# Two layout edits, five more side-by-side products per MLP, a split bias table and a final layer norm that works in PSUM

## The chip, the cores and the metric

The kernel runs on one NeuronCore of one Trainium2 chip. The time is device microseconds of that core, from launch to end; lower is better. Runs are shown as medians, and the profile is of one execution with its own time.

## The reference

A two-layer decoder trunk over 512 tokens of width 1024, all in float32. Layer 0 mixes with multi-head latent attention (8 heads, compressed keys and values, rotary part). Layer 1 mixes with grouped-query attention in a sliding window of 128 with a sink per head and a relative-position bias that is looked up in a 32x16 table. After each mixer and after each MLP comes a residual and a layer norm:

```python
def _mlp(x, w_up, w_down):
    h = jax.nn.relu(x @ w_up)          # 1024 -> 4096
    return (h * h) @ w_down            # 4096 -> 1024
...
for l in range(DEPTH):                 # DEPTH = 2
    y = _mla(x, ...) if l < 1 else _swa(x, ..., k_band, v_band, rel_bias)
    x = _layernorm(alpha * x + y, ln_mix_g[l], ln_mix_b[l])
    x = _layernorm(alpha * x + _mlp(x, mlp_w_up[l], mlp_w_down[l]), ln_mlp_g[l], ln_mlp_b[l])
```

The two MLPs hold most of the arithmetic.

## The kernel before, in words

**Precision.** Float32 operands are split into two parts of a reduced matmul type (fp32r): a high part `h` (ACT copies and rounds) and a low part `l` (DVE or POOL subtracts the high part from the value). A product is three passes of matmuls: high by high, high by low, low by high. `split` (lines 79 to 92) makes the parts, `three` lists the passes of one 128-row chunk, `by_pass` sorts a list of chunks by pass, and `group` (line 113) issues the matmuls and fixes their order in TensorE's program.

**The MLP.** The 4096 hidden features are worked in four blocks `q` of 1024. The up product (weights by tokens) of a block, and the down product of the first three, are done by a scheme for 2x2 block matrices that needs seven smaller products in place of eight. The products have the numbers 1, 2, 5, 3, 6, 7, 4; in the step strings `U'5` is the fifth up product of the next block and `D5` the fifth down product of this one. The order of the steps is written out in `FIRST_STEPS`, `SECOND_STEPS`, `STEPS` and `LAST_STEPS`. Blocks 2 and 3 run `U'1 D5 U'2 D3 U'5 ...`, block 0 runs `U'1 U'2 U'5 U'3 U'6 ...`. There are two MLPs, so each block occurs twice in a run. The last block's down product is done in the ordinary way (class `TokMajor`, method `finish`).

**An up product** has 128x128 weights as the stationary operand and 256 tokens of a factor of x as the moving one. Its two weights are `i`, the two halves of the output of each `j`, the chunks of the contraction `k` (4). There are two ways to issue it:

- plain (`up`): for each `(i, j, k)` three matmuls of 256 columns, 48 in all, into half a PSUM bank; `up_out` evacuates once per `i`, 512 columns at a time;
- side by side (`up_side`, lines 749 and 753): one matmul of 512 columns, the high weight by the high and the low part of x next to each other, and one of 256 columns, the low weight by the high part of x into the first half: 32 matmuls in all, one whole bank for each `(i, j)`; `side_out` (lines 786 and 787) evacuates each bank with an ACT copy of one half and a DVE add of the other.

`SIDE_BY_SIDE` says which products of which block go the second way: before, products 5 and 3 of blocks 1, 2 and 3. Products 1 and 2 share their banks (product 2 adds to what product 1 left).

**The factors of x** lie in tiles `xtb` of shape `[128, 2, 4, 256]`: part (high, low), chunk k, token. The 512-column moving operand of `up_side` is `src.both(n)[:, :, k, :]`: two runs of 256 elements, 1024 elements apart.

**Scratch.** Tag `uv` has three buffers: in block 0 two hold the sums `a` and `b` of the factors of x until the factors 6 and 7 are split, and one holds `u`. PSUM has six banks of tag `mm` and two of tag `tr`.

**The order of the work.** TensorE's matmuls and the weight loads by DMA keep program order (`keep_in_program_order`). ACT, DVE and POOL are ordered by a planner that takes ready instructions by priority from its own model of time. Each of these engines then runs its list in order.

**The bias table** (`bias_bands`, line 1032) is one plain float32 matmul of the 33x16 table by a 33x384 one-hot matrix; the result goes through DRAM and back as bands, which layer 1 reads much later.

**Values** (`values` of the first layer) are six matmuls of 512 columns for each token tile: for each of two chunks the passes high-high, high-low (low weights `wl`), low-high.

**The end.** `finish` of the last MLP evacuates the last token tile (t = 3) in chunks of 512, 256 and 256 columns: `add_last` adds the bank to x in SBUF and counts the statistics. `layer_norm` then aggregates, has POOL raise the variance to -1/2 (line 419), meanwhile subtracts the mean and multiplies by g over 1024 columns (line 442), and last multiplies by that and adds b in two halves (line 446), each followed by its DMA to the output.

Of the kernel before, what the change touches and what calls it, by code (L numbers as in the profile page):

```python
# [10 lines left out]
F32R = mybir.dt.float32r  # L11
AF = mybir.ActivationFunctionType
ALU = mybir.AluOpType
# [3 lines left out]
P = 128  # L17
D = 1024
S = 512
NT = S // P  # L20
# [6 lines left out]
SQH, SKVH, SHD = 16, 4, 64  # L27
# [6 lines left out]
BANDW = 384  # L34
POOL_O, POOL_SO = (0, 2), (0, 1, 2, 3)
WARM = 18

SIDE_BY_SIDE = {0: (), 1: (5, 3), 2: (5, 3), 3: (5, 3)}
PAIRED = (1, 2, 3, 4, 5, 6, 7)

ON_POOL = ("w_h", "w_o", "w_sq", "w_so")
# [12 lines left out]
def build(tc, nc, io, out):  # L54
    with ExitStack() as top:
        cp = top.enter_context(tc.tile_pool(name="cp", bufs=1))
        wp = top.enter_context(tc.tile_pool(name="wp", bufs=1))
        xp = top.enter_context(tc.tile_pool(name="xp", bufs=1))
# [7 lines left out]
        def nm(s):  # L66
            n_names[0] += 1
            return f"{s}_{n_names[0]}"

        def bank(cols=512, tag="mm", bufs=6):  # L70
            return ps.tile([P, cols], F32, tag=tag, bufs=bufs, name=nm(tag), padded_shape=[P, 512])
# [4 lines left out]
        def f32(ap):  # L76
            return ap.bitcast(F32)
# [23 lines left out]
        def pe(ins):  # L101
            tc.keep_in_program_order(ins)
# [3 lines left out]
        def pin(ins):  # L106

            if pinned[0]:
                pe(ins)

        def group(dst, pairs, first=True, last=True, **kw):
            for i, (st, mv) in enumerate(pairs):
                pe(nc.tensor.matmul(  # L113
                    dst, st, mv, start=first and i == 0, stop=last and i == len(pairs) - 1, **kw
                ))

        def three(sh, sl, mh, ml):
            return [(sh, mh), (sh, ml), (sl, mh)]

        def by_pass(chunks):  # L120

            return [chunk[n] for n in range(3) for chunk in chunks]
# [6 lines left out]
        def tiles_of_weights(aside=None):  # L129

            if aside:
                return aside()
            wh = wp.tile([P, 1024], F32R, tag="wh", bufs=4, name=nm("wh"))
            wl = wp.tile([P, 1024], F32R, tag="wl", bufs=4, name=nm("wl"))
            return wh, wl
# [222 lines left out]
        b = bank()  # L358
# [6 lines left out]
        def pieces(kp):  # L365
            return both[kp][:, 0:1024].rearrange("p (j c) -> p j c", j=2), both[kp][:, 1024:1664].rearrange("p (j c) -> p j c", j=2)
# [13 lines left out]
        for kp in range(4):  # L380
            x, weight = pieces(kp)
            wh, wl = tiles_of_weights()
            for j in (slice(0, 1), slice(1, 2)) if kp == 0 else (slice(0, 2),):
                w = lambda tile: tile[:, 0:640].rearrange("p (j c) -> p j c", j=2)[:, j]
                k = slice(2 * (kp % 2) + j.start, 2 * (kp % 2) + j.stop)
# [22 lines left out]
        relb = cp.tile([33, SQH], F32, name="relb")  # L408
# [14 lines left out]
        xs = [None] * NT  # L423
# [7 lines left out]
        def layer_norm(t, gb, dst, within=None):  # L431

            x = xs[t]
            mv = sp.tile([P, 2], F32, tag="mv", bufs=4, name=nm("mv"))
            pin(nc.vector.bn_aggr(mv, stats[t]))
            stats[t] = None
            v = sp.tile([P, 1], F32, tag="v", bufs=8, name=nm("v"))
            pin(nc.vector.tensor_scalar(v, mv[:, 1:2], LN_EPS, None, ALU.add))  # L438
            r = rsqrt_of(v)
            if within:  # L440
                within()
            pin(nc.vector.scalar_tensor_tensor(x, x, mv[:, 0:1], gb[:, 0, :], ALU.subtract, ALU.mult))
            n = 2 if dst is None and t == NT - 1 else 1
            for i in range(n):
                c = slice(i * D // n, (i + 1) * D // n)
                pin(nc.vector.scalar_tensor_tensor(x[:, c], x[:, c], r, gb[:, 1, c], ALU.mult, ALU.add))
                if dst is None:
                    nc.sync.dma_start(out[t * P : (t + 1) * P, c], x[:, c])
# [116 lines left out]
        stats = [None] * NT  # L565

        def count(t, c):

            n = 256 if t == NT - 1 else 512
            if stats[t] is None:  # L570
                stats[t] = sp.tile([P, D // n, 6], F32, tag="bn", bufs=4, name=nm("bn"), padded_shape=[P, 4, 6])
            for i in range(c.start // n, c.stop // n):
                pin(nc.vector.bn_stats(stats[t][:, i, :], xs[t][:, i * n : (i + 1) * n]))
# [4 lines left out]
        def add_plain(t, c, b):  # L578
            nc.vector.tensor_add(xs[t][:, c], b, xs[t][:, c])  # L579

        def add_scaled_last(t, c, b):
            add_scaled(t, c, b)
            count(t, c)

        def add_last(t, c, b):
            add_plain(t, c, b)
            count(t, c)

        def feat_major(src, w, dst, cols=slice(0, S), ks=range(KD), order=lambda chunks: sum(chunks, [])):
            wh, wl = w  # L590
# [55 lines left out]
        class XFactors(Factors):  # L646
# [6 lines left out]

            def both(self, n):
                if n not in self.tiles:
                    self.tiles[n] = xp.tile([P, 2, 4, 256], F32R, tag="xt", bufs=8, name=nm("xtb"))
                return self.tiles[n]

            def part(self, n, p):
                if n in PAIRED:  # L660
                    return self.both(n)[:, p]
                at = {1: (0, 0), 2: (0, 1), 5: (1, 0), 3: (1, 1), 6: (2, 0), 7: (2, 1), 4: (3, p)}[n]
                tile = (at[0], p if n != 4 else 0, "")
                if tile not in self.tiles:
                    self.tiles[tile] = xp.tile([P, 2, 4, 256], F32R, tag="xt", bufs=8, name=nm(("xth", "xtl")[p]))
                return self.tiles[tile][:, at[1]]
# [34 lines left out]
        def mlp(src, gb, dst, mp):  # L701
# [17 lines left out]
            class Block:  # L719
# [18 lines left out]
                def side(self, n):  # L738
                    return n in SIDE_BY_SIDE[self.q]

                def up_side(self, n, w):

                    key = own_bank.get(n, n)
                    for i, (wh, wl) in enumerate(w):
                        for j in range(2):
                            b = self.bank(("U", key), (i, j))
                            for k in range(4):
                                c = slice(j * 512 + k * P, j * 512 + (k + 1) * P)
                                pe(nc.tensor.matmul(  # L749
                                    b.rearrange("p (a b) -> p a b", a=2), wh[:, c], src.both(n)[:, :, k, :],  # L750
                                    start=n not in (2, 4) and k == 0, stop=False, skip_group_check=True,
                                ))
                                pe(nc.tensor.matmul(  # L753
                                    b[:, 0:256], wl[:, c], src.part(n, 0)[:, k, :],
                                    start=False, stop=k == 3, skip_group_check=True,
                                ))
                            self.side_out(n, i, j, b)
                        if n in (2, 6, 7, 4):
                            self.up_out(n, i)
                        if (self.q, i) == (0, 0) and n in (1, 2):  # L760
                            with tc.high_priority():
                                src.turn(n + 1)
# [155 lines left out]
            b = blocks[NFF - 1]  # L918
# [27 lines left out]
        with tc.tile_pool(name="mla", bufs=1) as mp:  # L946
# [3 lines left out]
            ckv_h = mp.tile([P, 2, S], F32R, name="ckv_h")  # L950
            ckv_l = mp.tile([P, 2, S], F32R, name="ckv_l")
# [57 lines left out]
            for kp in range(4):  # L1009
                wh, wl = weights("w_kv")  # L1010
# [16 lines left out]
            def bias_bands():  # L1027
                ohot, es = qrot[:, 0, :], qrot[:, 1, :]
                with tc.issue_after(small.ins):
                    nc.sync.dma_start(ohot[:33, :BANDW], io["oh"])  # L1030
                eb = bank()
                nc.tensor.matmul(eb[:SQH, :BANDW], relb, ohot[:33, :BANDW], start=True, stop=True)
                nc.scalar.activation(es[:SQH, :BANDW], eb[:SQH, :BANDW], AF.Copy)
                nc.sync.dma_start(ed, es[:SQH, :BANDW])
                e = ed[:, :]
                skew = bass.AP(tensor=e.tensor, offset=e.offset + 127, ap=[[BANDW, SQH], [-1, P], [1, 256]])
                nc.sync.dma_start(band, skew)
# [51 lines left out]
            def values(w, t):  # L1089
                wh, wl = w  # L1090
                tk = slice(t * P, (t + 1) * P)
                b = bank()
                for c in range(2):
                    cc = slice(c * 512, (c + 1) * 512)
                    group(b, three(ckv_h[:, c, tk], ckv_l[:, c, tk], wh[:, cc], wl[:, cc]), c == 0, c == 1)
                split(v_h[-1][:, t, :], v_l[-1][:, t, :], b)

            heads = [{} for _ in range(H)]
# [45 lines left out]
            for t in range(NT):  # L1144
                tk = slice(t * P, (t + 1) * P)
                b = bank()
                for r in range(3):
                    wh, wl = ws[r // 2]
                    c = slice((r % 2) * 512, (r % 2 + 1) * 512)
# [107 lines left out]
        gb = lambda: load_gb(io["ln_mix_g"][0], io["ln_mix_b"][0])  # L1257
# [188 lines left out]
        gb = lambda: load_gb(io["ln_mix_g"][1], io["ln_mix_b"][1])  # L1446
# [115 lines left out]
```

## Time and profile before

| what | value |
|---|---|
| median of 3 runs | 995.35 us (994.9 to 995.58) |
| profiled execution, its own time | 995.34 us |
| its span, first to last instruction | 993.1 us |
| mean granted TensorE clock | 0.998 |
| busy: PE, DVE, ACT, POOL | 983.4, 783.4, 569.7, 247.1 us |

The span is from the first to the last instruction; the 2.24 us between it and the profiled execution's time lie around it. Busy times are unions of an engine's instructions. A matmul's start is measured and its end is modelled, so what a matmul costs in a full stream is read from the distance between starts, or from the length of a piece of the chain divided by its count.

### The profile page before, as it was taken

What the parts mean: (1) busy time and instruction counts of PE and PEld (TensorE: products, weight loads), DVE (VectorE), ACT (ScalarE), POOL (GpSimd) and SP (SyncE); (2) the same over time, 40 slices, a digit from 0 to 9 for tenths busy, and PEclk for the clock granted to TensorE, in tenths of its full rate; (3) what the DMA queues carried; (4) which work ended last, traced back from release to release, by engine and by line L of the source; (5) the groups of instructions that cost most, each with busy time, mean ns of one, the idle gap of its engine ahead of it and who ended that gap; (6) DMA issues with size and microseconds to landing.
All of it is one profiled execution on the core that took longest, in us unless ns stands there. A gap on an engine that the chain in (4) does not pass through costs nothing.

```text
span 993.1 us, 15619 instructions
## 1 busy us (share of the span) xinstructions
PE 983.4 (99%) x5944; PEld 880.0 (89%) x5944; DVE 783.4 (79%) x1288; ACT 569.7 (57%) x895; POOL 247.1 (25%) x267
## 2 busy tenths in 40 slices
PE   9999999999999999999999999999999999999996
PEld 9888888999899889888899988889988998998986
DVE  6589857988878879896685678688996987888846
ACT  5557644467647647646146688546674664765710
POOL 1242101312212212210025675332131122023002
PEclk9999999999999999999999999999999999999999
DMA  7431126399889977963223211439798798797332
GB/s 262 133 100 43 64 107 191 96 221 230 154 181 233 179 171 213 227 112 126 108 75 108 85 65 54 169 65 235 213 187 193 175 208 179 165 263 142 80 127 85
DMA packets 60246, 149.54 MB, mean 151 GB/s; under 512 B 5211, under 2 KB 9740, under 8 KB 60172
## 3 DMA queue, kind: packets, MB, share of 16 engines
q0 software_dynamic: 24320, 58.73, 32.7%
q1 hardware_dynamic: 35564, 89.49, 26.6%
q8 instruction: 47, 0.77, 0.3%
q10 hardware_dynamic: 288, 0.33, 0.1%
q14 instruction: 27, 0.22, 0.1%
HBM read 146.41 MB, written 4.22 MB: 152 GB/s over the span
## 4 chain that ended last, share of the span: by engine, by line
PE 98%; DVE 1%; issue 0%; ACT 0%; POOL 0%; POOLq 0%; DVEq 0%
PE mm L113 83%; PE tr L113 5%; PE mm L749 5%; PE mm L753 2%; PE tr L1201 1%; PE tr L1384 1%; PE tr L678 1%; PE tr L1386 1%; PE tr L457 0%; PE mm L1125 0%; PE tr L979 0%; POOLq L1558 0%; POOL rs L419 0%; ACT p L1364 0%; DVE mm L1180 0%
## 5 line engine op out<-in xcount | busy, mean ns | idle before, releaser
L113 PE MATMUL mm<-wh,fac 128*128 128x512 f32 (+1 forms) x944 | 283.6, 386 | 0.0
L81 ACT ACTIVATE wh<-wq 128x1024 fp32r<-128x1024 f32 x164 | 173.6, 1060 | 169.6 <-PE mm L113 97.6
L89 DVE TENSOR_TENSOR wl<-wq,wh 128x1024 fp32r<-128x1024 f32 x164 | 199.2, 1220 | 55.6 <-ACT wh L81 55.1
L113 PEld LDWEIGHTS mm<-wh,fac 128*128 128x128 f32 x944 | 175.5, 188 | 35.5 <-DVE fac L89 0.6
L113 PE MATMUL mm<-wl,fac 128*128 128x512 f32 (+1 forms) x472 | 173.2, 386 | 0.0
L113 PE MATMUL mm<-xtb,wh 128*128 128x256 f32 x1024 | 172.2, 283 | 0.0
L113 PEld LDWEIGHTS mm<-xtb,wh 128*128 128x128 f32 x1024 | 152.4, 192 | 0.9
L198 POOL DMA_DIRECT2D wq<-in_up x64 | 77.6, 1222 | 252.4 <-DVE wl L89 181.7
L81 ACT ACTIVATE wh<-raw 128x1024 fp32r<-128x1024 f32 (+2 forms) x81 | 81.9, 1015 | 81.5 <-PE mm L113 59.4
L113 PE MATMUL mm<-xtb,wl 128*128 128x256 f32 x512 | 126.6, 283 | 0.0
L113 PEld LDWEIGHTS mm<-wl,fac 128*128 128x128 f32 x472 | 88.7, 188 | 17.1
L89 DVE TENSOR_TENSOR wl<-raw,wh 128x1024 fp32r<-128x1024 f32 (+2 forms) x59 | 70.7, 1207 | 34.8 <-ACT wh L81 34.5
L113 PEld LDWEIGHTS mm<-xtb,wl 128*128 128x128 f32 x512 | 90.2, 192 | 0.0
L198 POOL DMA_DIRECT2D wq<-in_down x48 | 42.0, 875 | 193.0 <-DVE wl L89 188.3
L419 POOL TENSOR_TENSOR rs<-v,half 128x1 f32<-128x1 f32 x24 | 28.7, 1197 | 190.7 <-DVE v L438 155.5
L87 POOL TENSOR_TENSOR wl<-raw,wh 128x256 fp32r<-128x256 f32 (+1 forms) x72 | 54.3, 791 | 65.6 <-ACT wh L81 65.6
L749 PE MATMUL mm<-xtb,wh 128*128 128x512 f32 x192 | 68.3, 398 | 0.0
L753 PE MATMUL mm<-xtb,wl 128*128 128x256 f32 x192 | 53.9, 281 | 0.0
L113 PE MATMUL mm<-wh,oh 128*128 128x512 f32 x128 | 50.9, 398 | 0.0
L113 PE MATMUL mm<-wh,ol 128*128 128x512 f32 x128 | 50.1, 391 | 0.0
L113 PE MATMUL mm<-wl,oh 128*128 128x512 f32 x128 | 49.9, 390 | 0.0
L579 DVE TENSOR_TENSOR x<-mm,x 128x512 f32<-128x512 f32 (+1 forms) x53 | 35.6, 675 | 13.8 <-PE mm L113 13.5
(235 smaller groups left out, 1996.6 us busy)
## 6 DMA issues: line engine op xcount, KB each, us to landing
wq<-in_up POOLq DMA_DIRECT2D x64, 512.0 KB, 8.0
wq<-in_down POOLq DMA_DIRECT2D x48, 512.0 KB, 7.2
wq<-in_up SPq DMA_DIRECT2D x32, 512.0 KB, 5.6
raw<-in_down SPq DMA_DIRECT2D x28, 512.0 KB, 6.2
wq<-in_down SPq DMA_DIRECT2D x24, 512.0 KB, 7.8
raw<-in_up SPq DMA_DIRECT2D x16, 512.0 KB, 4.7
raw<-in_w_o SPq DMA_DIRECT2D x8, 512.0 KB, 3.2
raw<-in_w_so SPq DMA_DIRECT2D x8, 512.0 KB, 3.5
```

The source lines that it names most:

```text
L81: high = nc.scalar.activation(dst_h, src, AF.Copy)
L87: low = engine.tensor_sub(dst_l[:, c : c + n], src[:, c : c + n], f32(dst_h[:, c : c + n]))
L89: low = (engine or nc.vector).tensor_sub(dst_l, src, f32(dst_h))
L113: pe(nc.tensor.matmul(dst, st, mv, start=first and i == 0, stop=last and i == len(pairs) - 1, **kw))
L198: nc.gpsimd.dma_start(half(a, jp), chunk(*more, jp), accum_op=ALU.add)
L419: nc.gpsimd.tensor_tensor(r, v, half, ALU.pow)
L579: nc.vector.tensor_add(xs[t][:, c], b, xs[t][:, c])
L678: pe(nc.tensor.transpose(pt[:, a, :], xs[t][:, k * P : (k + 1) * P], ident))
L749: pe(nc.tensor.matmul(b.rearrange("p (a b) -> p a b", a=2), wh[:, c], src.both(n)[:, :, k, :], start=n not in (2, 4) and k == 0, stop=Fals ...
L753: pe(nc.tensor.matmul(b[:, 0:256], wl[:, c], src.part(n, 0)[:, k, :], start=False, stop=k == 3, skip_group_check=True,))
L1201: pe(nc.tensor.transpose(pt[:, kb * P : (kb + 1) * P], p[:, kb * P : (kb + 1) * P], ident))
L1384: pe(nc.tensor.transpose(pt[:, a, 0:P], p[:, kb, P:256], ident))
```

## The change

Six edits:

1. `SIDE_BY_SIDE`: products 1 and 2 of blocks 2 and 3, and product 5 of block 0, are issued side by side too (ten more products in the two MLPs, beside twelve that were).
2. The factors' tiles become `[128, 4, 2, 256]` (chunk, part, token), so that the 512-column moving operand is one run of 512 elements; the 256-column ones stay runs of 256.
3. The bias table's matmul is done in fp32r: DVE copies the one-hot matrix and splits the table, and two matmuls (`group`, in program order) take the place of the float32 one.
4. `values`: the passes are sorted over both chunks, those with the low weights last.
5. In the last MLP, the two 256-column chunks of the last tile are added up in their PSUM banks, and the statistics are taken there; the mean is then subtracted from the banks into x.
6. The last tile's second half is finished and sent first, then the first half, whose mean is subtracted after that in the program's text.

```diff
-SIDE_BY_SIDE = {0: (), 1: (5, 3), 2: (5, 3), 3: (5, 3)}
+SIDE_BY_SIDE = {0: (5,), 1: (5, 3), 2: (1, 2, 5, 3), 3: (1, 2, 5, 3)}
...
-            pin(nc.vector.scalar_tensor_tensor(x, x, mv[:, 0:1], gb[:, 0, :], ALU.subtract, ALU.mult))
-            n = 2 if dst is None and t == NT - 1 else 1
-            for i in range(n):
-                c = slice(i * D // n, (i + 1) * D // n)
+            ends = [(slice(0, D), x)]
+            if dst is None and t == NT - 1:
+                for c, b in held:
+                    nc.vector.scalar_tensor_tensor(x[:, c], b, mv[:, 0:1], gb[:, 0, c], ALU.subtract, ALU.mult)
+                ends = [(slice(512, D), None), (slice(0, 512), x[:, :512])]
+            for c, from_ in ends:
+                if from_ is not None:
+                    pin(nc.vector.scalar_tensor_tensor(x[:, c], from_, mv[:, 0:1], gb[:, 0, c], ALU.subtract, ALU.mult))
                 pin(nc.vector.scalar_tensor_tensor(x[:, c], x[:, c], r, gb[:, 1, c], ALU.mult, ALU.add))
                 if dst is None:
                     nc.sync.dma_start(out[t * P : (t + 1) * P, c], x[:, c])
...
         def add_last(t, c, b):
-            add_plain(t, c, b)
-            count(t, c)
+            if t == NT - 1 and c.stop - c.start == 256:
+                held.append((c, b))
+                nc.vector.tensor_add(b, b, xs[t][:, c])
+                nc.vector.bn_stats(stats[t][:, c.start // 256, :], b)
+            else:
+                add_plain(t, c, b)
+                count(t, c)
...
-                    self.tiles[n] = xp.tile([P, 2, 4, 256], F32R, tag="xt", bufs=8, name=nm("xtb"))
+                    self.tiles[n] = xp.tile([P, 4, 2, 256], F32R, tag="xt", bufs=8, name=nm("xtb"))
...
-                    return self.both(n)[:, p]
+                    return self.both(n)[:, :, p]
...
-                                    b.rearrange("p (a b) -> p a b", a=2), wh[:, c], src.both(n)[:, :, k, :],
+                                    b, wh[:, c], src.both(n)[:, k].rearrange("p a b -> p (a b)"),
...
+                one, both_ = (mp.tile([P, S], F32R, tag=tag, bufs=2, name=nm(tag)) for tag in ("qh", "ql"))
+                parts_ = both_[:33, : 2 * SQH]
+                nc.vector.tensor_copy(one[:33, :BANDW], ohot[:33, :BANDW])
+                nc.vector.tensor_copy(parts_[:, :SQH], relb)
+                nc.vector.tensor_sub(parts_[:, SQH:], relb, f32(parts_[:, :SQH]))
                 eb = bank()
-                nc.tensor.matmul(eb[:SQH, :BANDW], relb, ohot[:33, :BANDW], start=True, stop=True)
+                group(eb[:SQH, :BANDW], [(parts_[:, i * SQH : (i + 1) * SQH], one[:33, :BANDW]) for i in range(2)])
...
+                chunks = []
                 for c in range(2):
                     cc = slice(c * 512, (c + 1) * 512)
-                    group(b, three(ckv_h[:, c, tk], ckv_l[:, c, tk], wh[:, cc], wl[:, cc]), c == 0, c == 1)
+                    hh, hl, lh = three(ckv_h[:, c, tk], ckv_l[:, c, tk], wh[:, cc], wl[:, cc])
+                    chunks.append((hh, lh, hl))
+                group(b, by_pass(chunks))
```

## Rows read from the trace of the kernel before

**Rows 1.** The page: busy time and share of the span; the chain by engine.

```profile
PE 983.4 (99%) x5944; PEld 880.0 (89%) x5944; DVE 783.4 (79%) x1288; ACT 569.7 (57%) x895; POOL 247.1 (25%) x267
...
PE 98%; DVE 1%; issue 0%; ACT 0%; POOL 0%; POOLq 0%; DVEq 0%
```

**Rows 2.** The chain in order of time, 255 to 345 us: start, length, what.

```profile
259.72 0.23 PE mm L749
...
260.06 0.23 PE mm L749
...
260.41 0.24 PE mm L749
...
260.77 0.23 PE mm L749
...
261.47 0.24 PE mm L749
...
265.36 10.90 PE mm L113 x48
...
287.38 5.75 PE tr L113 x48
```

**Rows 3.** Stretches U'1, D5, U'2, D3: length, busy PE, PEld, DVE, ACT, POOL; clock, DMA.

```profile
315.39:321.14 5.75, 5.75 (x49) 5.74 (x48) 5.73 (x6) 2.61 (x3) 1.76 (x2) 1.00 1.09 287
321.14:326.61 5.47, 5.47 (x26) 4.52 (x25) 4.29 (x5) 4.51 (x5) 0.00 (x0) 1.00 1.10 227
326.61:332.37 5.76, 5.76 (x50) 5.75 (x49) 5.76 (x6) 3.55 (x4) 1.72 (x2) 1.00 0.70 122
332.37:337.83 5.46, 5.46 (x26) 4.51 (x25) 2.30 (x4) 3.67 (x4) 2.41 (x2) 1.00 1.07 193
```

**Rows 4.** Groups by shape: line, engine, operation, count | busy, mean ns | idle before.

```profile
L787 DVE TENSOR_TENSOR a<-mm,a 128x256 f32<-128x256 f32 x24 | 9.5, 416 | 0.0
...
L819 ACT ACTIVATE uv<-mm 128x512 f32<-128x512 f32 x16 | 9.3, 584 | 2.9 <-PE mm L113 2.7
...
L786 ACT ACTIVATE a<-mm 128x256 f32<-128x256 f32 x24 | 9.0, 375 | 3.3 <-PE mm L753 3.3
```

**Rows 5.** DVE in order of time, U'1 to U'2 of block 2.

```profile
319.90 1.22 DVE L89 TENSOR_TENSOR wl<-raw,wh 128x1024 fp32r<-128x1024 f32 x1
322.32 1.23 DVE L89 TENSOR_TENSOR wl<-raw,wh 128x1024 fp32r<-128x1024 f32 x1 [1.20 <-ACT wh L81]
```

**Rows 6.** DVE in order of time, U'5 to U'6 of block 0, first MLP.

```profile
201.34 1.82 DVE L89 TENSOR_TENSOR xtb<-uv,xtb 128x512 fp32r<-128x512 f32 x2
...
212.43 1.23 DVE L89 TENSOR_TENSOR wl<-wq,wh 128x1024 fp32r<-128x1024 f32 x1 [1.32 <-ACT wh L81]
```

**Rows 7.** The chain in order of time around the bias table's matmul.

```profile
27.64 0.75 PE mm L1032 x2
...
30.52 4.17 PE mm L113 x24
```

**Rows 8.** DVE and PEld in order of time, after that matmul and at the values.

```profile
30.85 0.75 DVE L981 SCALAR_TENSOR_TENSOR ckv_l<-tr,gkv,ckv_h 128x512 fp32r<-128x512 f32 x1 [4.33 <-ACT ckv_h L980]
...
36.85 1.40 DVE L1078 CAST kr_both<-tr 64x512 fp32r<-64x512 f32 x2
...
39.57 0.19 PEld L113 LDWEIGHTS mm<-wl,ckv_h 128*128 128x128 f32 x1 [0.40 <-DVE wl L89]
```

**Rows 9.** DVE and POOL in order of time at the end of the kernel.

```profile
982.69 0.42 DVE L579 TENSOR_TENSOR x<-mm,x 128x256 f32<-128x256 f32 x1
...
983.22 1.28 DVE L446 SCALAR_TENSOR_TENSOR x<-x,rs,gb 128x1024 f32<-128x1024 f32 x1
...
986.77 1.27 DVE L442 SCALAR_TENSOR_TENSOR x<-x,mv,gb 128x1024 f32<-128x1024 f32 x1
986.93 1.52 POOL L419 TENSOR_TENSOR rs<-v,half 128x1 f32<-128x1 f32 x1 [3.75 <-DVE v L438]
...
988.49 1.41 DVE L446 SCALAR_TENSOR_TENSOR x<-x,rs,gb 128x512 f32<-128x512 f32 x2 [0.44 <-POOL rs L419]
```

More of the change, by code (lines that the diff above doesn't have):

```diff
@@ L583, in add_scaled_last @@
             count(t, c)
+        held = []
         def add_last(t, c, b):
-            add_plain(t, c, b)
-            count(t, c)
+            if t == NT - 1 and c.stop - c.start == 256:
[5 more added lines that the diff above has]
+                count(t, c)
         def feat_major(src, w, dst, cols=slice(0, S), ks=range(KD), order=lambda chunks: sum(chunks, [])):
```

## The prediction

> **What bounds the kernel now.** I read the page's busy times and chain first. TensorE is busy for 99% of the span, and 98% of the chain that ends last is its work, against 79% for DVE and 57% for ACT [rows 1]. So a nanosecond less of matmul is a nanosecond less of time, as long as ACT and DVE still deliver. Second I read the chain in order of time, because busy times of overlapping matmuls don't tell what one costs in a full stream. [...] Then groups by shape for prices, and short stretches around each of the small edits.
>
> **Step 1, the matmul rate of the products.** A plain up product is 48 matmuls in 5.75 us, 0.120 us for each, with no hole between them [rows 2]. A side-by-side one runs from the first L749 at 259.72 to the next work at 265.36: 5.64 us for 16 pairs, 0.353 us a pair [rows 2]. A 512-column matmul with one contiguous run as its moving operand takes 10.90 / 48 = 0.227 us [rows 2]. In a pair, 0.353 less 0.120 leaves 0.233 us for the 512-column matmul that reads two runs: 6 ns more. The first pair takes 0.34 us, the second 0.35, the third 0.36, and two later ones together 0.70 [rows 2]. A loss that starts after two pairs and then stays looks like a reader that falls behind a little with each operand and had some slack at first, so I put it down to the second run of the read. No row shows a long stream of alternating 512 and 256 columns with contiguous reads, so the price of the new pair is bounded: not under 0.227 + 0.113 (the first pair's 0.34), not over today's 0.353. I take 0.227 + 0.120 = 0.347, the sum of the two rates in long streams. A product is then 16 x 0.347 = 5.55 us.
>
> - Ten products that were plain, five in each MLP: 10 x (5.75 - 5.55) = 2.0 us. If the layout does nothing: 10 x (5.75 - 5.64) = 1.1 us.
> - Twelve products that were side by side: 12 x (5.64 - 5.55) = 1.1 us, or nothing.
>
> Together 3.1 us, bounds 1.1 and 4.7 (22 products at 16 x 0.34 = 5.44).
>
> **Step 2, what the ten products hand to DVE and ACT.** In blocks 2 and 3 each of products 1 and 2 gets four DVE adds of 256 columns at 0.416 us that the plain way did not have, 3.3 us a block; ACT does eight copies at 0.375 in place of four operations on 512 columns at 0.584, and one whole-tile relu beyond them, some 1.7 us more [rows 4]. Room: in U'1, D5, U'2, D3 of block 2 DVE is busy 18.1 of 22.4 us, full in U'1 and U'2 and free for 1.2 and 3.2 us in D5 and D3; ACT is busy 14.3 of 22.4 [rows 3]. 18.1 + 3.3 = 21.4 still fits, at 96%. The adds fall due at the end of each bank, so half of them slide into D5 and D3. What a late DVE would hold up next is the split of U'2's own low weights: it ends at 322.32 + 1.23 = 323.55 [rows 5], and U'2 begins at 326.61 [rows 3], so 3.1 us of cover against 1.7 us of adds from U'1. Banks: products 1 and 2 now hold four of six in place of two, and D5 takes the other two, freed by D'2 during U'1. U'2 must find U'1's banks read out, with the 5.47 us of D5 between [rows 3]; the next product 5 needs them back after D3, 5.46 us later. Cost at nothing; if the cover went, up to 1.7 us at each of eight places, 13 us.
>
> **Block 0's product 5** now needs its scratch `v` at once, while the three `uv` buffers hold `a`, `b` and `u`. `a` comes free after the split of factor 6, 201.34 + 1.82 = 203.2 us [rows 6], about when the product ends, so its four banks wait until then. Product 3 needs two banks, which are the two that product 2 leaves, and product 6 uses the other tag; product 7 starts two products later. The four adds, 1.7 us, go into a stretch where DVE is full until about 211, but the next weight splits then wait 1.3 us for ACT (for a buffer), not for DVE [rows 6]. Cost at nothing; if it were not hidden, 1.7 us in each MLP.
>
> **Step 3, the bias table.** The float32 matmul takes 0.75 us of the chain [rows 7]. Two fp32r matmuls of 384 columns at the 4.17 / 24 = 0.174 us of their neighbours [rows 7] take 0.35: 0.4 us less. The three DVE operations are no wider than 384 columns; the nearest row, a rounding copy of 512 columns, is 0.70 us, so under 2.1 us in all, probably near 0.9. DVE stands idle for 4.33 us up to 30.85, around that matmul [rows 8]. The matmuls are now held in order, so every later one waits if the copies are late; planned into the idle time just before, a copy could cost its own 0.7. Bounds: 0.4 gained, 0.7 lost; I take the gain, as the inputs are there long before.
>
> **Step 4, values.** At the first tile the load of the low weights waits 0.40 us for DVE's split [rows 8]. With the low weights in the last third, four matmuls of 0.227 stand ahead of them, 0.9 us. Part of the wait would have lain under the matmul before it; between 0 and 0.40 is won, I take 0.3.
>
> **Step 5, the end.** The chain is add, statistics, the power on POOL (986.93 + 1.52 = 988.45), two halves of 0.70, DMA. The number and width of operations before the power do not change. Under the power there now lie two subtracts of 256 columns from banks, and the subtract of the first half if the planner pulls it ahead: two of some 0.42 and one of 0.70 after 986.77 end at 988.3, just under the 988.49 at which DVE resumes [rows 9]. That the planner pulls ready work ahead is seen one tile earlier: the add of the last tile (982.69) runs before the final step of the tile before it (983.22) [rows 9]. If it does not, the last DMA is 0.7 us later. I take 0, bounds 0.2 gained and 0.7 lost.
>
> **The sum.** 3.1 + 0.4 + 0.3 + 0 = 3.8 us. The profiled execution took 995.34 us, within 0.01 of the median; its span is 993.1. The forecast is 991.5 us, 0.38% less. A difference under 0.2%, 2.0 us, cannot be told from none here: faster is below 993.35, slower above 997.35.
>
> **The rivals.**
>
> *The layout does nothing.* The pair's 6 ns come from alternating long and short matmuls, not from the second run. For it: the first pairs with the same two runs show no loss, and nothing in the trace separates the two explanations. Against it: a plain stream and a stream of 512 columns each hold their rate. The time: 995.34 - 1.1 - 0.4 - 0.3 = 993.5, within 0.2%. [...]
>
> *The vector engines can't carry it, and the kernel gets slower.* Place: U'2 of blocks 2 and 3, where DVE is already at 5.76 of 5.76 us [rows 3]. If the planner puts U'1's adds ahead of the low-weight splits and the evacuation of product 2 ahead of those for D3, DVE's lag grows by up to 1.7 us at each. It decides from the point where the lag exceeds the 3.1 us of cover; once past it, 1.7 us at four blocks is 6.7 us, less the 3.8 won: 998.2 us. Against it: the 1.2 and 3.2 us that DVE has free in D5 and D3 let a lag be worked off before the next product adds to it [rows 3].
>
> *The gain is given back to the weights.* Faster products ask for weights sooner; the DMA engines are at 1.1 of their share in U'1 and D5 [rows 3]. A product that waits as long as it was shortened gains nothing: the ten and twelve products together return between a half and all of 3.1 us, and the time is 993.0 to 994.6, say 993.9. Against it: the chain through these blocks has no hole today [rows 2].
>
> **How the numbers follow.** Forecast 0.55 (its own range, with the small steps at their bounds, 990.6 to 992.7); layout without effect 0.20; weights 0.14; vector engines 0.11. Faster: the forecast's 0.55 and a third of the weights case, and a small part of the layout case (its lower bounds): 0.62. Slower: 0.08, most of the third rival. Same: 0.30. The range goes from the forecast's low end to cover the layout and weights cases with the end's 0.7 us lost: 990.5 to 994.9; above it lies the vector case, below it nearly nothing.
>
> **What would show it.** L749 groups: start to start of pairs 0.347 (step 1 right) or 0.353 (layout without effect); products 1 and 2 of blocks 2 and 3 at 5.55 us; matmuls down by 160 from 5944 [rows 1]. No PEld wait for `wl` over 0.3 us at U'2, D3 and U'5 of blocks 2 and 3, and none for banks at U'3 and U'7 of block 0. The table's two matmuls at 0.35 us, the low-weight wait at 39.6 us gone, and the last DVE operation ending about 1.4 us after the power. A pair at 0.353 us, or a DVE that is full through D5 and D3, would make the forecast wrong.

## The result, and the profile after

The changed kernel takes 1002.05 us (median of six runs, 999.56 to 1003.63) against 995.21 us before (six runs, 994.52 to 995.8): a ratio of 1.0067, 95% interval 1.0057 to 1.0077. It is slower by 6.8 us where 3.8 us less were forecast, and the time lies above the range. The profiled execution took 1000.8 us, its span is 998.6.

The page after: busy times, and the chain by engine [rows 1].

```profile
PE 983.6 (99%) x5784; PEld 870.2 (87%) x5784; DVE 797.7 (80%) x1333; ACT 575.7 (58%) x923; POOL 245.9 (25%) x267
...
PE 91%; ACT 3%; DMA 2%; DVE 2%; issue 1%; POOL 0%; SPq 0%; DVEq 0%; ACTq 0%
```

The 160 matmuls are gone, and yet PE is as long busy; the chain leaves TensorE for 9% where it left it for 2%. The chain in order of time in U'1 of block 2 (start, length, what), which answers to [rows 2]:

```profile
317.41 0.23 PE mm L760
317.64 0.12 PE mm L764
317.76 0.23 PE mm L760
...
323.06 5.46 PE mm L113 x24
```

A product is still 323.06 - 317.41 = 5.65 us, a pair still 0.353: the contiguous operand gave nothing. The four stretches of block 2 (length, busy PE, PEld, DVE, ACT, POOL; clock, DMA share, GB/s), which answer to [rows 3]:

```profile
317.41:323.06 5.65, 5.65 (x34) 4.91 (x33) 5.65 (x7) 3.24 (x6) 1.76 (x2) 1.00 1.10 276
323.06:328.52 5.46, 5.46 (x25) 4.50 (x25) 5.37 (x9) 4.21 (x5) 0.00 (x0) 1.00 1.10 222
328.52:334.16 5.64, 5.64 (x33) 4.90 (x33) 5.64 (x7) 4.13 (x7) 1.72 (x2) 1.00 0.61 100
334.16:339.62 5.46, 5.46 (x26) 4.50 (x25) 3.90 (x7) 2.62 (x4) 2.41 (x2) 1.00 1.02 191
```

TensorE has no hole here. DVE is busy for 20.6 of 22.2 us, up from 18.1; it carried products 1 and 2.

The place that the forecast costed at nothing looks different. PEld (TensorE's weight loads) at down product 1 of block 0 (D1, written `D'1` in `FIRST_STEPS`, where it stands behind `D'2` and `U'4`), first MLP (start, length, operation, in brackets the wait ahead of it and who ended it), first in the kernel before, then in the changed one:

```profile
230.59 1.03 PEld L113 LDWEIGHTS mm<-xtb,wl 128*128 128x128 f32 x8
231.56 0.31 PEld L113 LDWEIGHTS mm<-wh,fac 128*128 128x128 f32 x2
...
232.37 0.88 PEld L113 LDWEIGHTS mm<-wh,fac 128*128 128x128 f32 x4
```

```profile
230.06 1.03 PEld L113 LDWEIGHTS mm<-xtb,wl 128*128 128x128 f32 x8
231.97 0.30 PEld L113 LDWEIGHTS mm<-wh,fac 128*128 128x128 f32 x2 [0.87 <-ACT fac L81]
...
234.34 0.76 PEld L113 LDWEIGHTS mm<-wh,fac 128*128 128x128 f32 x4 [1.62 <-DVE fac L89]
```

TensorE waits twice, for the high and for the low part of the factor, and again in the second MLP. ACT just ahead of that, before and after:

```profile
223.81 2.01 ACT L846 ACTIVATE a<-a 128x1024 f32<-128x1024 f32 x2 [3.14 <-DVE a L836]
225.73 1.04 ACT L81 ACTIVATE wh<-wq 128x1024 fp32r<-128x1024 f32 x1
226.67 1.99 ACT L847 ACTIVATE a<-a 128x1024 f32<-128x1024 f32 x2
...
229.51 1.04 ACT L81 ACTIVATE fac<-a 128x1024 fp32r<-128x1024 f32 x1
```

```profile
224.22 1.06 ACT L81 ACTIVATE wh<-wq 128x1024 fp32r<-128x1024 f32 x1 [4.01 <-PE mm L113]
225.19 1.99 ACT L857 ACTIVATE a<-a 128x1024 f32<-128x1024 f32 x2
227.09 1.04 ACT L81 ACTIVATE wh<-wq 128x1024 fp32r<-128x1024 f32 x1
228.03 1.99 ACT L858 ACTIVATE a<-a 128x1024 f32<-128x1024 f32 x2
...
230.88 1.04 ACT L81 ACTIVATE fac<-a 128x1024 fp32r<-128x1024 f32 x1
```

The operations are the same, the list is not: a weight split that waits 4.01 us for a buffer now stands ahead of the relu, and the high part starts 1.4 us later. DVE, before and after:

```profile
229.64 1.23 DVE L89 TENSOR_TENSOR wl<-wq,wh 128x1024 fp32r<-128x1024 f32 x1
230.78 1.22 DVE L89 TENSOR_TENSOR fac<-a,fac 128x1024 fp32r<-128x1024 f32 x1
231.92 0.69 DVE L844 TENSOR_TENSOR a<-mm,uv 128x512 f32<-128x512 f32 x1
```

```profile
231.33 0.69 DVE L855 TENSOR_TENSOR a<-mm,uv 128x512 f32<-128x512 f32 x1 [1.05 <-PE mm L113]
231.94 1.22 DVE L89 TENSOR_TENSOR wl<-wq,wh 128x1024 fp32r<-128x1024 f32 x1
233.07 1.22 DVE L89 TENSOR_TENSOR fac<-a,fac 128x1024 fp32r<-128x1024 f32 x1
```

The low part fell behind a bank's second read that itself waits for TensorE, and behind a weight split: 2.3 us later.

Block 0's product 5 itself is no shorter: from 196.89 to 202.64 it takes 5.75 us, where the plain one took 5.76. Ahead of it stands a wait for the low part of its factor, which the wide matmul reads at once and the plain product only in its second pass (over the span: waits in all, how many, the longest):

```profile
PEld mm L760 <- DVE xtb L89: 0.6, 2, 0.3
```

The small edits came as forecast. The table's chain is 0.3 us shorter, the low-weight wait of [rows 8] is gone. At the end (DVE, then POOL, against [rows 9]):

```profile
992.50 0.87 DVE L445 SCALAR_TENSOR_TENSOR x<-mm,mv,gb 128x256 f32<-128x256 f32 x2
993.28 0.74 DVE L449 SCALAR_TENSOR_TENSOR x<-x,mv,gb 128x512 f32<-128x512 f32 x1
993.94 1.41 DVE L450 SCALAR_TENSOR_TENSOR x<-x,rs,gb 128x512 f32<-128x512 f32 x2
```

```profile
992.66 0.55 POOL L419 TENSOR_TENSOR rs<-v,half 128x1 f32<-128x1 f32 x1 [3.76 <-DVE v L438]
```

The planner pulled the first half's subtract ahead, as argued, and the last two halves follow at once.

### The profile page after: what moved, and what is told of

It reads as the page before. It is cut to its first block, busy times and chain, and to the rows that moved or that the text cites. A ratio compares the mean times of both kernels' runs of the same rounds, so it can differ in the third digit from the quotient of the medians.

```text
span 998.6 us, 15400 instructions
## 1 busy us (share of the span) xinstructions
PE 983.6 (99%) x5784; PEld 870.2 (87%) x5784; DVE 797.7 (80%) x1333; ACT 575.7 (58%) x923; POOL 245.9 (25%) x267
## 4 chain that ended last, share of the span: by engine, by line
PE 91%; ACT 3%; DMA 2%; DVE 2%; issue 1%; POOL 0%; SPq 0%; DVEq 0%; ACTq 0%
PE mm L113 71%; PE mm L760 8%; PE tr L113 5%; PE mm L764 4%; ACT wh L81 1%; PE tr L1220 1%; DMA raw<-in_w_so 1%; DMA raw<-in_w_o 1%; PE tr L1403 1%; PE tr L689 1%; DVE wl L89 1%; PE tr L1405 0%; DMA xw<-in_xT 0%; ACT a L857 0%; POOL wl L87 0%
## 5 line engine op out<-in xcount | busy, mean ns | idle before, releaser
L760 PE MATMUL mm<-xtb,wh 128*128 128x512 f32 x352 | 125.4, 399 | 0.1
L113 PE MATMUL mm<-xtb,wh 128*128 128x256 f32 x704 | 117.5, 283 | 0.0
L113 PEld LDWEIGHTS mm<-xtb,wh 128*128 128x128 f32 x704 | 104.0, 192 | 0.4
L764 PE MATMUL mm<-xtb,wl 128*128 128x256 f32 x352 | 98.8, 281 | 0.0
L113 PE MATMUL mm<-xtb,wl 128*128 128x256 f32 x352 | 85.9, 283 | 0.0
L760 PEld LDWEIGHTS mm<-xtb,wh 128*128 128x128 f32 x352 | 66.1, 188 | 16.7 <-DVE xtb L89 0.6
L764 PEld LDWEIGHTS mm<-xtb,wl 128*128 128x128 f32 x352 | 66.5, 189 | 0.8
L113 PEld LDWEIGHTS mm<-xtb,wl 128*128 128x128 f32 x352 | 61.5, 192 | 0.0
```

What stands on the lines that cost most here:

```text
L113: pe(nc.tensor.matmul(dst, st, mv, start=first and i == 0, stop=last and i == len(pairs) - 1, **kw))
L760: pe(nc.tensor.matmul(b, wh[:, c], src.both(n)[:, k].rearrange("p a b -> p (a b)"), start=n not in (2, 4) and k == 0, stop=False, skip_gro ...
L764: pe(nc.tensor.matmul(b[:, 0:256], wl[:, c], src.part(n, 0)[:, k, :], start=False, stop=k == 3, skip_group_check=True,))
```

## The experiments

All were timed in five rounds beside the kernel before, which stood at 995.1 to 995.4 us each time. Times are medians; the ratio to before is given with its 95% interval.

**Which part costs.** Three kernels: the changed one without block 0's fifth product; the one before with that alone; the small edits alone (old `SIDE_BY_SIDE`, old layout).

```diff
-SIDE_BY_SIDE = {0: (5,), 1: (5, 3), 2: (1, 2, 5, 3), 3: (1, 2, 5, 3)}
+SIDE_BY_SIDE = {0: (), 1: (5, 3), 2: (1, 2, 5, 3), 3: (1, 2, 5, 3)}   # e1, from after
+SIDE_BY_SIDE = {0: (5,), 1: (5, 3), 2: (5, 3), 3: (5, 3)}   # e2, from before
```

> The changed kernel with product 5 of block 0 issued the plain way again; all else as changed. Theory: that product alone makes the planner order the first block's first down factor late, two holes of 0.74 and 1.45 us in TensorE's work in each MLP, 4.4 us a run; without it the holes are gone and the time is 4.4 us under the changed kernel's, 997.7 us or less (the sum of the other terms that the trace of the changed kernel shows, 0.9 for products 1 and 2, 0.3 for the table, 0.3 for values, 0.3 for the end, would give 993.4). Rival: the time is lost to DVE's added work in blocks 2 and 3 or to late weight transfers; then it stays near 1002.

> The kernel before with only product 5 of block 0 side by side. Theory: the same two holes at the first down product of block 0 in both MLPs, so 995.2 + 4.4 - 0.2 = 999.4 us. Rival (blocks 2 and 3, or the small edits, are the cause): 995.0, no difference.

> The kernel before with only the small edits: bias table in fp32r, values sorted by pass, end in banks and second half first; products and layout as before. Theory: 0.3 + 0.3 + 0.3 us won, 994.3. Rival: the planner, moved by three more DVE operations early, orders something later worse and the edits cost time: 996 to 998.

Measured: 993.49 us (0.9984, 0.9976 to 0.9993); 1003.45 us (1.0078, 1.0066 to 1.0091); 994.33 us (0.9994, 0.9985 to 1.0003). Block 0's fifth product costs 8.3 to 8.6 us by itself, nearly twice what the holes of the trace explain; all the rest together gains 1.7.

**The layout alone.**

```diff
-xp.tile([P, 2, 4, 256], ...)   both(n)[:, :, k, :]
+xp.tile([P, 4, 2, 256], ...)   both(n)[:, k]
```

> The kernel before with the new layout of the factors' tiles alone. Theory (the second run of the read costs nothing): 995.2 us, a pair of matmuls still 0.353 us from start to start, a side-by-side product 5.64 us. Rival (part of what the changed kernel gained without block 0's fifth product is the layout): 994.2 us, and products shorter than 5.64 us.

Measured: 995.01 us (0.9999, 0.9990 to 1.0007). The layout does nothing.

**The order within a bank.** If the 6 ns of a pair come from alternating, they go when equal matmuls stand together. From e1:

```diff
 for k in range(4):
     pe(nc.tensor.matmul(b, wh[:, c], ...))
+for k in range(4):
     pe(nc.tensor.matmul(b[:, 0:256], wl[:, c], ...))
```

> The changed kernel without block 0's fifth product, and in each bank of a side-by-side product the four matmuls of 512 columns stand first and the four of 256 after them. Theory (the 6 ns of a pair come from alternating long and short): a bank takes 4 x 0.227 + 4 x 0.120 = 1.39 us in place of 1.41, a product 5.55 in place of 5.64, and twenty products give 1.8 us: 991.7 us. Rival (the 6 ns belong to the matmul of 512 columns in these products or to the change from one bank region to another, whatever the order): 993.5 us.

Measured: 993.13 us (0.9978, 0.9969 to 0.9987), the fastest kernel of all; against e1 0.36 us, inside the intervals. Its chain in U'1 of block 2:

```profile
314.63 0.91 PE mm L760 x4
315.54 0.47 PE mm L766 x4
316.01 0.93 PE mm L760 x4
...
320.22 0.93 PE mm L113 x4
```

A product is 5.59 us, about half of the way from 5.64 to 5.55: some half of the 6 ns goes with the alternation. The rest stays with the wide matmuls: of the product's four groups of four in a row the first takes 0.91 us and the others 0.93, 0.2325 each, against 0.227 in the long stream of [rows 2]. Why is not settled.

**The lists, two places held.** From the changed kernel: the relu ahead of the weight split on ACT, the factor's low part ahead of product 4's second read on DVE.

```diff
+with behind((relu,)): grown(...)        # the weight split
+with behind((self.low1,)): nc.vector.tensor_add(self.quarter(done)[:, pairs], of(7), ...)
```

> The changed kernel with product 5 of block 0 still side by side, and two orders written out: on ACT the split of one weight comes after the relu of the first factor's quarters (as in the kernel before), and on DVE the low part of block 0's first down factor comes before product 4's second evacuation (as before). Theory (the order, not the product, costs the time): the holes of 0.74 and 1.45 us shrink to under 0.3 in sum in each MLP, and the time is about that of the run without the product, within 0.5 us. Rival (the product's evacuation work itself delays the factor): still 1.5 us or more lost in each MLP, 1001 to 1002.

Measured: 999.79 us (1.005, 1.0037 to 1.0062). The waits at D1 of the first MLP shrank to 0.53 and 0.67 us (0.80 and 0.67 in the second) and did not go, since other splits had moved ahead of the factor; and two waits that e1 does not have stand in the layer between, near 586 and 647 us, as in the changed kernel. The order is part of it, but this was no clean test.

**The matmuls with the low part last**, in D1 alone.

```diff
+for low in (False, True):
+    for t in range(2):
+        ...
+        group(self.bank(("D", key), t), pairs of this pass, not low, low)
```

> The changed kernel, block 0's fifth product side by side as in it; only the first down product of block 0 issues its matmuls in another order: those with the high part of the factor for both token tiles first (16 matmuls of 0.227 us, 3.6 us), those with the low part last. Theory (what costs is TensorE waiting for the two parts of that factor, and the clock that falls after it): the second hole, 1.45 us in each MLP, goes and the first of 0.74 stays: 993.5 + 1.5 = 995.0, up to 996.5 with other waits of up to 1.5 us that the changed kernel's trace has elsewhere; no run above 997. Rival (the fifth product costs by its own work on DVE and ACT, which shows at whatever comes next): 1000 to 1002 us, the hole only moves to a later product.

Measured: 998.54 us (997.16 to 1000.21; 1.0035, 1.0023 to 1.0048). The second hole is gone from the trace, the first stays at 0.88, and the profiled run is 997.2, but the median is 2 us above the upper end of what was expected (996.5). Something else costs.

**The holes filled with work.** The lists of ACT, DVE and POOL are the changed kernel's, operation for operation; TensorE is kept busy in the two waits.

```diff
+for _ in range(4): pe(nc.tensor.matmul(b, wh[:, 0:P], wh[:, 0:512], start=True, stop=True))
 group(b, passes[:4], True, False)
+for _ in range(7): pe(nc.tensor.matmul(bank of t=1, wh[:, 0:P], wh[:, 0:512], start=True, stop=True))
 group(b, passes[4:], False, False)
```

> The changed kernel; the two stretches in which TensorE waits for block 0's first down factor are filled with matmuls whose result is overwritten (four of 512 columns ahead of the product, seven after its first four matmuls), so TensorE works there and the lists of DVE, ACT and POOL are the changed kernel's. Theory (the holes make the granted clock fall afterwards, and that is the difference between the changed kernel's runs near 1000 and near 1003.4 us): the holes' own time stays, 993.5 + 4.4 + some 1 to 2 of other waits = 999 to 1000 us, up to 0.5 more where the fill is longer than the hole, with all runs in one group and the mean clock at 0.998. Rival (the clock falls for another reason): runs in two groups near 1000 and 1003.4 us, the latter with a mean clock of 0.994 to 0.996.

Measured: 999.14 us, all five runs between 998.52 and 999.39, each with a mean granted clock of 0.998 (1.0038, 1.0025 to 1.0051). Of the changed kernel's six runs, the three at 999.6 to 1000.8 us have a mean clock of 0.998 or 0.999, the three at 1003.3 to 1003.6 one of 0.994 to 0.996; 0.003 of 1000 us is the 3 us between them. (Some 2 us that the changed kernel loses in the layer between, explained below, are not in e9's trace.) What a lower clock looks like is in the profile of e2, D1 of the second MLP (stretch, busy PE, PEld, DVE, ACT, POOL; clock, DMA):

```profile
714.00:716.00 2.00, 1.32 (x8) 0.83 (x6) 1.60 (x2) 1.83 (x3) 0.51 (x1) 1.00 1.04 315
716.00:718.00 2.00, 0.84 (x4) 0.48 (x3) 2.00 (x3) 1.97 (x3) 1.20 (x1) 0.91 1.06 253
718.00:720.00 2.00, 2.00 (x7) 1.52 (x6) 0.50 (x1) 0.27 (x1) 1.20 (x1) 0.50 1.05 251
720.00:722.00 2.00, 2.00 (x8) 1.63 (x7) 0.93 (x2) 0.00 (x0) 0.00 (x0) 0.74 1.03 243
```

After two holes, of 0.88 and 1.60 us, TensorE comes back at a granted clock of 0.50. Reckoned from the clock of the three stretches, 2 x (0.09 + 0.50 + 0.26) = 1.7 us are lost behind a wait that is already paid for. It does not follow every time: the same two holes in the first MLP of this run passed at 1.00. With the holes filled it did not happen in five runs.

**The factor with priority.** From e8: block 0's fifth product side by side again, the factor issued first; and the same with block 1's products 1 and 2.

```diff
+with tc.high_priority():
     relu, square of a11
+    self.factor(1)
```

> The kernel with wide matmuls first (993.1 us) and block 0's fifth product side by side again, but the relu, the square and the split of the one factor that the first down product needs are issued with high priority right after product 6, so that on ACT and DVE two weight splits stand behind the factor's parts that stood ahead of them. Theory (side by side in block 0 costs only because the planner's lists made this factor late): no hole at the first down product, the fifth product 0.1 to 0.15 us shorter in each MLP: 992.9 us, 992.6 to 993.4, mean clock 0.997 to 0.999. Rival (the product's own eight operations more on ACT and DVE are too many there, so the late work only moves to the weights): over 995 us with waits for weight splits of 0.5 us and more.

> The kernel of the run before this one, with products 1 and 2 of block 1 side by side too. Theory (the vector engines have room, as in blocks 2 and 3): four products at 0.14 us less, 0.6 us: 992.3 us. Rival (in block 1 the two products follow each other without a down product between, so DVE gets eight adds in one stretch and falls behind): 993.5 to 1000 us, with waits for weight splits or factors after product 2 of block 1.

Measured: 1017.43 us and 1017.19 us (1.0226, 1.0212 to 1.024; 1.0219, 1.0206 to 1.0233). Both theories fell, by a fault of the edit: the factor of the down product that comes first (D2) was now issued after that of D1 and came 9 us late in each MLP. So block 1 stays untested. The price of a hole shows well, though (e10, same columns):

```profile
220.00:224.00 4.00, 0.20 (x2) 0.00 (x0) 4.00 (x7) 0.98 (x2) 0.00 (x0) 1.00 0.51 177
224.00:228.00 4.00, 0.00 (x0) 0.00 (x0) 1.05 (x1) 4.00 (x5) 0.00 (x0) 0.65 0.42 97
...
230.00:232.00 2.00, 2.00 (x6) 1.52 (x6) 0.59 (x1) 0.00 (x0) 0.00 (x0) 0.50 1.01 406
```

**All lists held.** From e8 with block 0's fifth product: `issue_after` at six places, until the lists of ACT and DVE differed from e8's only by the product's own operations.

```diff
+with behind({2: ("relu",), 3: ("square",), 4: ("high",)}.get(n_w)):     # n-th weight split after product 7
     high = nc.scalar.activation(dst_h, src, AF.Copy)
+with behind({1: ("last7",), 4: ("low",)}.get(n_w)):
     low = nc.vector.tensor_sub(dst_l, src, f32(dst_h))
```

> The kernel with wide matmuls first (993.1 us) and block 0's fifth product side by side again, this time with the lists of ACT and DVE held by hand to the order that they have without it: they differ from that kernel's lists only by the product's own four copies on ACT and four adds on DVE in each MLP (and by where two subtractions read their operand). Theory (only the order of the lists makes the first down factor late): no hole over 0.3 us at the first down product, clock 0.997 to 0.999, 992.9 us, 992.5 to 993.5. Rival (the eight operations themselves, 1.7 us on DVE and 1.5 us on ACT, push the factor back whatever the order): a hole of 0.4 to 1.7 us at the first down product of both MLPs, 994 to 997 us.

Measured: 995.19 us (993.76 to 997.73; 1.0003, 0.9994 to 1.0012). PEld at D1:

```profile
229.50 1.03 PEld L120 LDWEIGHTS mm<-xtb,wl 128*128 128x128 f32 x8
230.46 0.31 PEld L120 LDWEIGHTS mm<-wh,fac 128*128 128x128 f32 x2
...
231.27 0.88 PEld L120 LDWEIGHTS mm<-wh,fac 128*128 128x128 f32 x4
```

No wait, in either MLP: the holes came from the order alone. But 2 us remain. The waits of the span name two that e8 does not have:

```profile
PEld mm L120 <- ACT p L1399: 1.1, 1, 1.1
...
PEld mm L120 <- DVE wl L95: 1.1, 1, 1.1
```

Both go back to the output weights `w_so` of the layer between, which land late because two issues on SP (the engine that issues these DMAs) are long: 1.24 and 1.43 us, where e8's same issues take 0.41 and 0.43. In the first case ACT, which computes `p`, stands behind the split of those weights:

```profile
582.06 1.06 ACT L86 ACTIVATE wh<-raw 128x1024 fp32r<-128x1024 f32 x1 [1.89 <-DMA raw<-in_w_so]
```

SP around the two issues:

```profile
576.81 1.24 SPq L157 DMA_DIRECT2D raw<-in_w_so  x1
```

```profile
633.45 1.43 SPq L434 DMA_DIRECT2D gb<-in_ln_mix_g  x1
```

and the DMA queues in the microsecond from 576 to 577 (queue, packets, MB, share):

```profile
q8 instruction: 1, 0.02, 8.2%
```

This 16 KB packet, of the kind that the row calls "instruction" and this text program code, starts at 576.3, another at 633.3. Over all traces they come 12 to 37 us apart, half of them 18.5 to 24. In the changed kernel two such packets stand at 579.8 and 636.4, with issues of 1.05 and 1.28 us right there; in e4 and e7 likewise, where TensorE waits 1.3 and 0.9 us, and 0.6 and 1.1. In the kernel before, e1, e2, e8 and e9 none stands there, and both issues are short. A meeting does not always lengthen an issue: in the fifteen traces, 23 of the 99 issues of SP that start within 0.5 us of such a packet take 0.95 us or more; of the 2469 others (from 12 us on), 6 do.

**The code shifted.** First with more and smaller warm-up matmuls at the start, then by cutting 18 matmuls of block 0's down products in two.

```diff
-group(b[:, :256], [(zeros[:, :P], zeros)] * WARM)
+group(b[:, :128], [(zeros[:, :P], zeros[:, :128])] * (2 * WARM - 2))     # e13
```

> The kernel with block 0's fifth product and its lists held (995.2 us), with the 18 warm-up matmuls of 256 columns at its start cut into 34 of 128 columns: the same work, but 16 more matmuls in TensorE's program, as many as block 0's fifth product takes out of it. In the profiles the 16 KB packets of program code on DMA queue 8 come every 15 to 25 us; in the run before this one two of them start within 0.5 us of an issue on SP (576.3 to the output weights' transfer at 576.8, 633.3 to one at 633.4), that issue takes 1.2 and 1.4 us in place of 0.4, and TensorE waits 1.1 and 1.2 us for those weights; without block 0's fifth product they come at 571.6 and 629.5. Theory (the remaining 2 us are this meeting of a code packet with an issue, an accident of the program's length): the packets come 3 to 5 us earlier again, these issues take 0.4 us, and the time is 992.9 us, 992.4 to 993.6. Rival (the eight vector operations make the output weights late in another way): 994.5 to 996 us, the waits at 583.6 and 643.5 us stay.

```diff
+if (self.q, n, t) in ((0, 1, 0), (0, 2, 0), (0, 2, 1)) and i == 1:       # e14
+    for half_ in range(2):
+        cut = slice(half_ * 256, half_ * 256 + 256)
+        group(b[:, cut], [(st, mv[:, cut]) for st, mv in pairs], False, True)
```

> The kernel with block 0's fifth product and its lists held (995.2 us), where in each MLP 18 matmuls of 512 columns of block 0's first two down products are cut into two of 256 with the same weights, so TensorE's program is 18 matmuls longer. Price from the kernel before's rows: 18 x (2 x 0.120 - 0.227) = 0.23 us in each MLP, 0.5 us in all. Theory (what is left of the cost of block 0's fifth product once its factor is in time is the code packet that meets the output weights' issue): the two issues take 0.4 us again, no wait at 583.6 and 643.5 us, 992.9 + 0.5 = 993.4 us, 992.8 to 994.1. Rival (those waits were an accident of that one profile, and the median of 995.2 us has another cause): 995 to 996 us.

Measured: e13 998.25 us (1.0026, 1.0015 to 1.0038). Against e12's trace both waits are gone, 1.10 and 1.21 us, as expected; but the 34 small matmuls took 7.33 us (their weight loads) where 18 of twice the width had taken 3.81, and those behind them started 0.267 us apart up to 13 us, where e12's do so 0.147 apart from 5.5 us on: TensorE lost 5.2 us at the start. By its median the theory failed, for a reason of the edit's own. e14 has that price out: 993.33 us (992.9 to 994.19; 0.9982, 0.9973 to 0.9991), 993.4 expected. Its issue:

```profile
577.46 0.41 SPq L157 DMA_DIRECT2D raw<-in_w_so  x1
```

The packets stand at 571.8 and 629.6, and the lists of ACT, DVE and POOL are e12's, operation for operation. Against e12's trace TensorE gains 1.2 us at the first of the two places and 1.3 at the second. So the last 2 us were the meeting of a code packet with an issue. Both edits that made TensorE's program longer moved the packets off these two issues; what else sets their phase stays open.

## Why the prediction was wrong

**The step that failed** is "Block 0's product 5 ... Cost at nothing; if it were not hidden, 1.7 us in each MLP"; block 0's fifth product cost 8.3 to 8.6 us. It looked at whether the four adds fit and at what waits next in the old order. They fit: with the old order held, the product costs nothing at D1 (e12). But the lists of ACT and DVE are made by a planner from its own model of time, and a new product in block 0 gave new lists far behind it. Where the weight splits stand in them decides whether D1's factor is in time, and nothing in the argument asked for that. The bound of 1.7 us was wrong as well, as it priced the operations and not what a late factor sets off. Start times of the same matmuls in the traces of e1 and the changed kernel give the 7.5 us between these two profiled runs: 2.4 at D1 of either MLP, 2.1 at the layer between (0.7 near 586 and 1.4 near 647 us; nearly all of it the output weights that met a code packet, which is an accident of this program's length), 0.2 net up to 193 us, and 0.2 at block 0's product 5 in each MLP. The median lies 1.25 above the profiled run, as half of the runs carry the lower clock. That e2 comes to nearly the same, 8.3 us, is partly luck: its trace has no long issue at the output weights, but three of its five runs have a mean clock of 0.994, about two losses of 1.7 us.

**Step 1** had the wrong cause. The rival "The layout does nothing" was right on the layout: 5.65 us a product and 0.353 a pair with one run, 5.64 and 0.353 with two. Its own reason, the alternation, holds for about half of the 6 ns (e8: 5.59 us a product). Of the 3.1 us, the eight plain products of blocks 2 and 3 gave 8 x 0.11 = 0.9; block 0's two gave nothing (5.75 against 5.76 us, behind a wait of 0.3) and cost 8. The bound of 4.7 us for this step was a wrong sum: 10 x 0.31 + 12 x 0.20 is 5.5. The outcome does not hang on it.

**Step 2, blocks 2 and 3**: right, 20.6 us of DVE work against the 21.4 reckoned, and no wait. The rival "The vector engines can't carry it" named the right kind of mechanism, a planner's order that makes a part late, but the wrong block.

**Steps 3 to 5**: 0.3, 0.3 and 0.3 us against 0.4, 0.3 and 0; the last came from the power on POOL, which the forecast had at its old 1.52 us and which took 0.55. All but block 0 thus gives 0.9 + 0.9 = 1.8; e1 measured 1.7.

## What to carry to other kernels

Where a planner orders the vector engines, an edit's price is not the work that it adds but the lists that it produces: compare the planned order of each engine before and after, over the whole block, and look at what the next matmul waits for. A hole in TensorE can cost twice, once as the wait and once as the clock that comes back at half: in e2's second MLP 0.88 and 1.60 us of waits, and then 1.7. And when two microseconds stay unexplained at a place that the change does not touch, look at the DMA queues there: with a program of another length the code packets here moved from 576.3 and 633.3 us, where they met two issues (e12), to 571.8 and 629.6, clear of both (e14).

## What the hardware showed that was not expected

- The last power on POOL took 0.55 us, where that of the kernel before took 1.52 [rows 9], as all sixteen powers beside line 442 did there (1.46 to 1.53). In the first case DVE reads a PSUM bank and SBUF at the time, in the second two operands in SBUF. No run varies this alone, so the cause is not shown.
- Where a code packet of queue 8 met one of these issues on SP, the issue was 0.6 to 1.0 us longer: 1.05 and 1.28 us in the changed kernel, 1.24 and 1.43 in e12, against 0.41 and 0.43 in e8. The two meetings cost about 2 us: the median of e12 is 995.19 us, that of e14 993.33.
- At the start of the kernel a matmul of 128 columns takes as long as one of 256: e13's 34 and the 18 of the kernel before both start 0.213 us apart. The first row is e13's, the second e12's, whose last three matmuls already go faster: its 18 take 3.81 us, those of the kernel before 4.21.

```profile
1.10 7.33 PEld L120 LDWEIGHTS mm<-zeros 128*128 128x128 f32 x34 [1.10 <-POOL zeros L364]
```

```profile
1.10 3.81 PE L120 MATMUL mm<-zeros 128*128 128x256 f32 x18 [1.10 <-POOL zeros L364]
```
